# One step of a hybrid DeltaNet / attention network on one core: modulation loads in pieces, gate rows in two heads' memories, softmax scaling on GpSimd or DVE

## The chip, the core and the metric

The kernel runs on one core of a Trainium2 chip. The metric is the device time of one execution in microseconds (us); the time before is the median of 3 runs. Below, PE is TensorE's matmul queue and PEld its weight loads, DVE is VectorE, ACT ScalarE, POOL GpSimd, and SP the engine whose queue issues the DMAs.

## What is computed

Two layers of width 1024 over 384 tokens, 128 of context (`x_prompt`) and 256 latent (`x_sample`). Layer 0 mixes with a gated DeltaNet of 8 heads, layer 1 with windowed attention of 16 heads; each layer ends with a gated feed-forward block. All arithmetic is float32; large products are split into high and low parts and done as three float32r products. Cut to what matters here:

```python
m = silu(cvec) @ w_ada[i] + b_ada[i]              # modulation, (1024) @ (1024, 6144), for context and latent
shift, scale, gate, shift2, scale2, gate2 = split(m, 6)
h = rmsnorm(x, g) * (1 + scale) + shift
y = gated_delta_mixer(h) if i == 0 else attention(h)
x = x + gate * rmsnorm(y, g)
h = rmsnorm(x, g) * (1 + scale2) + shift2
x = x + gate2 * rmsnorm(conv_ffn(h), g)
...
p = softmax(concat([scores, sink]))[..., :-1]     # attention
o = p @ v
```

## The kernel before, in words

**Who sets the order.** The program is written as tasks (Python generators). A task asks for an engine (`yield "P"` for PE, "A" for ACT, "V" for DVE, "G" for POOL, "Q" for SP's queue), for buffers (`Slots`) or for an event; with several letters it takes the engine that can start it first. A planner (`Sched`, L101) plays this through with written-in costs and grants each engine to the task that could start earliest, then by priority (a small number is urgent). The order found is fixed in the program: every engine, SP among them, works through its own list in that order and waits on semaphores, so whatever stands behind a waiting instruction on its engine waits too. The planner lets DMAs through one after the other at 360 GB/s (`DBW`) with a fixed delay (`DL2`). It has no notion of one engine slowing another.

**The stages.** `begin` (L1818) computes the first modulation and starts layer 0's projections. `delta` (L1094) runs the DeltaNet: tiles of 128 output columns of the input projection (`fm`, L400: 24 matmuls of 384 tokens), and beside them one chain per head (`t_chain`, L1257). A chain loads the head's decay rows `dm` as a broadcast (`t_decay`, L1243), forms the matrix `N`, and inverts it in `t_inverse` (L1439), whose way goes through DRAM: `N` is written (`nd<-N`), its diagonal blocks read back (`tmp<-nd`, `X<-nd`), solved on POOL, written (`zd<-inv`) and read in another layout (`x<-zd`) before PE can go on. The convolution of a projected tile (`conv`, L444) frees the bank that the tile was in; `vf` is its output for v. `tm` (L857) does the output projection, holds the last weights back so that the token blocks finish one after the other, and then makes the transition: for each block `y` = result x gate (`t_gated`, L706), x is updated (`t_half`, L735) and multiplied with (1 + g) (`t_scale`, L752), and TensorE multiplies with a diagonal matrix of the norms (`diag,y`) and adds the shift (`t_quarter`, L758). `ffn` (L946) and `attention` (L1573) call the same `tm`.

**Modulation.** `w_ada` comes in 40 loads of 1 MB behind the first ones (`t_ada`, L514), each into one of the buffers in `self.ada`: two of its own at first (`ada`), later any memory that a stage lends (`lend`, L388). Two loads make one step of 512 columns (`t_mod`, L523; its matmuls are `ada,sc`, `head,sc` and so on), which is fitted in between other work with priority 9 or 20; steps 11 and 12, 16 to 18 and 22 and 23 are kept to fill the three transitions. The rows of gate and (1 + g) are written to DRAM (`gdram`, `adram`) and loaded back as broadcasts of 1 MB into all partitions (`t_rows`, L662). At the end of the DeltaNet this happens after the hook (L1142) has waited for every chain, given the chains' memory back and issued the reload of x, whose memory the chains use as scratch. The memories of heads 4 to 7 (`head`) are lent to the modulation when those heads are done (L1408 to 1411).

**Attention.** `t_unit` (L1704) handles two heads of one token block: scores, then a reduction with mask and sink on DVE, the exponentials on ACT, the sum's reciprocal `l`, and the scaling of `P` by it on DVE, one instruction per head (48 in all, 16 of 128 columns and 32 of 384). PE then transposes `P` (`ident,P`), the result is copied to `PT` by ACT or DVE, and multiplied with v.

Of the kernel before, what the change touches and what calls it, by code (L numbers as in the profile page):

```python
# [11 lines left out]
F32 = mybir.dt.float32  # L12
F32R = mybir.dt.float32r
BF16 = mybir.dt.bfloat16
AF = mybir.ActivationFunctionType
ALU = mybir.AluOpType

D = 1024
# [4 lines left out]
H = 8  # L23
# [29 lines left out]
DMIN = 0.06  # L53
DBW = 360.0
DQ = 0.47
SV = 0.0
# [44 lines left out]
class Sched:  # L101
# [17 lines left out]
    def set(self, ev):  # L119
        self.acts.append(lambda end: self._set(ev, end))  # L120

    def put(self, slots, *items):
# [142 lines left out]
class Net:  # L265
# [248 lines left out]
    def t_ada(self):  # L514
        for l, n, half in self.msrc:
            raw = yield self.ada, 1
            yield "Q"
            self.s.put(self.adaful, (raw, self.dma(raw, self.i["w_ada"][l, n, half])))

# [337 lines left out]
    def tm(self, act, ready, plan, l, w, tail, nxt, hook=None):  # L857
# [24 lines left out]
        for n, pieces in enumerate(plan):  # L882
            if n == (len(plan) - tail if hook else 0):
                pool = hook() if hook else self.pool
                if hook:
                    pool = yield from pool
                ctx["gate"] = pool.tile([128, 2, D], F32, name="gate"), Event()
                self.s.spawn(self.t_rows(self.gates[l, w], self.gdram[l][w], *ctx["gate"]), 3)
                if nxt is not None:
                    ctx["arow"] = pool.tile([128, 2, D], F32, name="arow"), Event()  # L890
                    ctx["diags"] = [pool.tile([128, 128], F32, name=f"diag{b}") for b in range(3)]
                    ctx["shift"] = [pool.tile([128, n], F32R, name=f"shift{n}{m}") for m, n in enumerate((128, 128, 16))], Event()
                    self.s.spawn(self.t_shift(self.AB[nxt], *ctx["shift"]), 3)
                    self.s.spawn(self.t_rows(self.AB[nxt], self.adram[nxt[0]][nxt[1]], *ctx["arow"]), 3)
            wt = yield self.wready, 1
# [198 lines left out]
    def delta(self, pool, nxt):  # L1094
        tc, i, s = self.tc, self.i, self.s
        with ExitStack() as late:
# [17 lines left out]
                   for n in range(NB)]  # L1114
# [6 lines left out]
            self.norms = Slots([dict(osb=t(f"osb{n}", [128, 3, 128]), **{k: t(f"{k}{n}", [128, 3]) for k in ("so", "rt", "rs")})  # L1121
                                for n in range(2)])
            self.odone = odone = [[Event()] for _ in range(H)]
            self.gateh, self.written = set(), set()
# [17 lines left out]
            def hook():  # L1142
# [8 lines left out]
                yield "Q"  # L1151
                self.load_x()
                return pp

# [102 lines left out]
    def t_chain(self, h, t):  # L1257
# [150 lines left out]
        if h < H - 4:  # L1408
            s.put(self.hslots, t)
        else:  # L1410
            self.lend(t["mem"].rearrange("p (j c) -> p j c", j=4))
# [292 lines left out]
    def t_unit(self, ti, b, q, done):  # L1704
# [4 lines left out]
        w = yield self.Ps, 1  # L1709
# [26 lines left out]
        for hh in range(2):  # L1736
            V.tensor_scalar(P[:, hh, :n], P[:, hh, :n], l2[:, hh:hh + 1], None, op0=ALU.mult)
        PT = []
# [230 lines left out]
```

## Time and profile before

| | us |
|---|---|
| runs | 1107.46, 1107.84, 1106.46 (median 1107.46) |
| the profiled execution, its own time | 1107.74 |
| its span, from the first to the last instruction | 1106.0 |
| PE busy in the span | 1062.2 (96%) |
| DVE, ACT, POOL busy | 696.2, 549.8, 235.0 |
| DMA moved | 177.86 MB, mean 161 GB/s |

Busy time is that in which an engine has an instruction in work. PE pipelines its matmuls, so a busy PE can still be at less than its peak. PEclk is the clock that was granted to TensorE as a share of 2.4 GHz, averaged over a stretch in which it can only be at 1.2 or 2.4. In a timeline, the number in brackets behind a row is how long the engine had stood idle before it and what ended that.

### The profile page before, as it was taken

Reading aid. Unit: us, or ns where it says so; the run is one execution under the profiler, and the core shown is the slowest. Engines: PE = TensorE matmul, PEld = TensorE weight load, DVE = VectorE, ACT = ScalarE, POOL = GpSimd, SP = SyncE. Lnnn points to the kernel's source line nnn. Section 1 sums busy time; section 2 is a strip of 40 time slices with the busy share of each in tenths; the row PEclk is TensorE's granted clock in tenths of the full one; section 3 lists DMA queues with packets and bytes.
Section 4 is the critical chain, followed back from the end, with each engine's and each line's share of the span. In section 5 each row is a group of like instructions: output and inputs, shape, how many; then the busy total and the mean of one; then the engine's idle time right before and its main releaser. Section 6 shows DMA issues by size and latency. Waiting matters only on the chain.

```text
span 1106.0 us, 19683 instructions
## 1 busy us (share of the span) xinstructions
PE 1062.2 (96%) x7397; PEld 927.4 (84%) x7397; DVE 696.2 (63%) x1685; ACT 549.8 (50%) x1127; POOL 235.0 (21%) x403
## 2 busy tenths in 40 slices
PE   6999899999998999999999999999999999999997
PEld 4887778899785999999988869776769999999886
DVE  5578656988546565656654456878577556566434
ACT  4576754767534444444543345566455444445422
POOL 0023545646202122222200021000031222221000
PEclk9999999999899999999999999998999999999999
DMA  9768664356345534533583346621514434335431
GB/s 364 279 224 293 189 193 127 104 167 204 96 166 223 199 126 132 196 120 128 169 316 126 113 133 220 212 95 41 192 35 142 132 118 132 126 123 172 129 119 57
DMA packets 73567, 177.86 MB, mean 161 GB/s; under 512 B 25816, under 2 KB 38744, under 8 KB 66432
## 3 DMA queue, kind: packets, MB, share of 16 engines
q1 hardware_dynamic: 73472, 176.61, 47.7%
q8 instruction: 58, 0.95, 0.3%
q14 instruction: 37, 0.30, 0.1%
HBM read 169.45 MB, written 7.13 MB: 160 GB/s over the span
## 4 chain that ended last, share of the span: by engine, by line
PE 81%; DMA 6%; DVE 5%; POOL 4%; issue 2%; ACT 1%; SPq 1%; DVEq 0%; POOLq 0%; ACTq 0%
PE bank L299 79%; PE bank L319 2%; POOL tmp L261 1%; DMA tmp<-nd 1%; DVE y L261 1%; POOL inv L261 1%; DMA gate<-gdram 1%; DMA nd<-N 1%; DMA x<-zd 1%; DMA ada<-in_w_ada 1%; DVE x L261 1%; DMA first<-in_w_ada 1%; SPq L324 1%; POOL stat L261 1%; DVE hlo L261 1%
## 5 line engine op out<-in xcount | busy, mean ns | idle before, releaser
L299 PE MATMUL bank<-hhi,whi 128*128 128x384 f32 x832 | 283.8, 341 | 4.1 <-DVE vf L261 2.8
L299 PE MATMUL bank<-hlo,whi 128*128 128x384 f32 x832 | 283.6, 341 | 0.2 <-DVE hlo L261 0.2
L299 PE MATMUL bank<-hhi,wlo 128*128 128x384 f32 x832 | 282.2, 339 | 0.0
L261 DVE TENSOR_TENSOR wlo<-raw,whi 128x1024 fp32r<-128x1024 f32 x151 | 184.9, 1225 | 64.1 <-ACT whi L261 64.0
L261 DVE SCALAR_TENSOR_TENSOR u<-bank,cw_ff,u 128x127 f32<-128x127 f32 x352 | 122.3, 410 | 145.3 <-ACT u L261 145.3
L261 ACT ACTIVATE whi<-raw 128x1024 fp32r<-128x1024 f32 x151 | 158.6, 1052 | 58.3 <-PE bank L299 46.8
L299 PEld LDWEIGHTS bank<-hhi,whi 128*128 128x128 f32 x832 | 156.7, 188 | 14.6 <-DVE vf L261 3.4
L299 PEld LDWEIGHTS bank<-hlo,whi 128*128 128x128 f32 x832 | 156.7, 188 | 4.2 <-issue 2.0
L299 PEld LDWEIGHTS bank<-hhi,wlo 128*128 128x128 f32 x832 | 156.7, 188 | 1.2 <-issue 0.8
L261 ACT ACTIVATE u<-bank,cw_ff 128x384 f32<-128x384 f32 x88 | 59.2, 673 | 177.2 <-PE bank L299 177.2
L261 POOL TENSOR_TENSOR g<-u 128x384 f32<-128x384 f32 x44 | 79.6, 1809 | 307.0 <-DVE u L261 276.6
L299 PE MATMUL bank<-whi,hhi 128*128 128x512 f32 (+1 forms) x246 | 96.7, 393 | 0.0
L299 PE MATMUL bank<-wlo,hhi 128*128 128x512 f32 (+1 forms) x246 | 94.1, 383 | 0.0
L299 PE MATMUL bank<-whi,hlo 128*128 128x512 f32 (+1 forms) x246 | 94.0, 382 | 0.0
L261 POOL TENSOR_TENSOR stat<-stat,mhalf 128x1 f32<-128x1 f32 x24 | 15.7, 656 | 253.0 <-DVE stat L261 253.0
L299 PE MATMUL bank<-hhi,wlol 128*128 128x384 f32 x200 | 67.9, 339 | 0.0
L299 PE MATMUL bank<-hlo,whil 128*128 128x384 f32 x200 | 67.7, 339 | 0.0
L299 PE MATMUL bank<-hhi,whil 128*128 128x384 f32 x200 | 67.7, 339 | 0.0
L261 DVE TENSOR_TENSOR wlol<-raw,whil 128x1024 fp32r<-128x1024 f32 x38 | 46.3, 1218 | 14.0 <-ACT whil L261 14.0
L299 PEld LDWEIGHTS bank<-whi,hhi 128*128 128x128 f32 x246 | 46.6, 190 | 9.6 <-issue 0.7
L299 PEld LDWEIGHTS bank<-whi,hlo 128*128 128x128 f32 x246 | 46.7, 190 | 9.2
L299 PEld LDWEIGHTS bank<-wlo,hhi 128*128 128x128 f32 x246 | 46.8, 190 | 8.0
(253 smaller groups left out, 1740.0 us busy)
## 6 DMA issues: line engine op xcount, KB each, us to landing
raw<-in_ffn_w_up SPq DMA_DIRECT2D x88, 512.0 KB
ada<-in_w_ada SPq DMA_DIRECT2D x32, 1024.0 KB
raw<-in_ffn_w_down SPq DMA_DIRECT2D x44, 512.0 KB
raw<-in_dn_w_in SPq DMA_DIRECT2D x29, 512.0 KB
first<-in_w_ada SPq DMA_DIRECT2D x6, 1024.0 KB
head<-in_w_ada SPq DMA_DIRECT2D x4, 1024.0 KB
raw<-in_dn_w_out SPq DMA_DIRECT2D x8, 512.0 KB
gate<-gdram SPq DMA_DIRECT2D x4, 1024.0 KB
```

Source lines behind the costliest of these rows:

```text
L261: return f(out, *a, **k)
L299: self.nc.tensor.matmul(out, lhsT, rhs, **kw)
L319: self.nc.tensor.transpose(out, src, ident)
L324: self.nc.sync.dma_start(out=out, in_=src)
```

## The change

1. A modulation load of 1 MB becomes four DMAs of 256 KB into the same buffer, and in the planner's time at least 1.5 us pass between the end of issuing one piece and the next of this task.
2. When heads 4 and 5 are done, their memories are no longer lent to the modulation; the rows of gate (into the first that finishes) and of (1 + g) (into the second) are loaded into them, as soon as these rows are in DRAM. The transition after the DeltaNet uses them. In the place where gate and (1 + g) had their own tiles, two buffers `adb` are made after the chains and lent to the modulation. The other transitions keep their own tiles.
3. The scaling of `P` asks for "VG": the planner gives each of the two instructions of a unit to DVE (as before) or to GpSimd, there as a product with a broadcast of the reciprocal.

```diff
@@ -52,6 +52,7 @@
 DL2 = 1.6
 DMIN = 0.06
 DBW = 360.0
+PIECES, PAUSE = 4, 1.5
 DQ = 0.47
 SV = 0.0
 ZD = 1
@@ -118,6 +119,9 @@
 
     def set(self, ev):
         self.acts.append(lambda end: self._set(ev, end))
+
+    def after(self, ev, time):
+        self.acts.append(lambda end: self._set(ev, end + time))
 
     def put(self, slots, *items):
         for i in items:
@@ -514,8 +518,14 @@
     def t_ada(self):
         for l, n, half in self.msrc:
             raw = yield self.ada, 1
-            yield "Q"
-            self.s.put(self.adaful, (raw, self.dma(raw, self.i["w_ada"][l, n, half])))
+            for j in range(0, 4, 4 // PIECES):
+                if j:
+                    yield pause
+                yield "Q"
+                c = slice(j, j + 4 // PIECES)
+                ev, pause = self.dma(raw[:, c, :], self.i["w_ada"][l, n, half][:, c, :]), Event()
+                self.s.after(pause, PAUSE)
+            self.s.put(self.adaful, (raw, ev))
 
     def mod_prio(self):
         return 0 if not self.started else 9 if self.mod_count < self.mod_goal or self.filling else 20
@@ -884,14 +894,18 @@
                 pool = hook() if hook else self.pool
                 if hook:
                     pool = yield from pool
-                ctx["gate"] = pool.tile([128, 2, D], F32, name="gate"), Event()
-                self.s.spawn(self.t_rows(self.gates[l, w], self.gdram[l][w], *ctx["gate"]), 3)
+                if hook:
+                    ctx["gate"], ctx["arow"] = self.lentrows
+                else:
+                    ctx["gate"] = pool.tile([128, 2, D], F32, name="gate"), Event()
+                    self.s.spawn(self.t_rows(self.gates[l, w], self.gdram[l][w], *ctx["gate"]), 3)
+                if nxt is not None and not hook:
+                    ctx["arow"] = pool.tile([128, 2, D], F32, name="arow"), Event()
+                    self.s.spawn(self.t_rows(self.AB[nxt], self.adram[nxt[0]][nxt[1]], *ctx["arow"]), 3)
                 if nxt is not None:
-                    ctx["arow"] = pool.tile([128, 2, D], F32, name="arow"), Event()
                     ctx["diags"] = [pool.tile([128, 128], F32, name=f"diag{b}") for b in range(3)]
                     ctx["shift"] = [pool.tile([128, n], F32R, name=f"shift{n}{m}") for m, n in enumerate((128, 128, 16))], Event()
                     self.s.spawn(self.t_shift(self.AB[nxt], *ctx["shift"]), 3)
-                    self.s.spawn(self.t_rows(self.AB[nxt], self.adram[nxt[0]][nxt[1]], *ctx["arow"]), 3)
             wt = yield self.wready, 1
             for k, _ in pieces:
                 yield full[k]
@@ -1120,6 +1134,7 @@
                                      R=t("R", [128, 2, 128]), sn=t("sn", [128, 2, 128]))])
             self.norms = Slots([dict(osb=t(f"osb{n}", [128, 3, 128]), **{k: t(f"{k}{n}", [128, 3]) for k in ("so", "rt", "rs")})
                                 for n in range(2)])
+            self.lentrows = []
             self.odone = odone = [[Event()] for _ in range(H)]
             self.gateh, self.written = set(), set()
             s.spawn(self.t_zero(nqs, works), 8)
@@ -1150,6 +1165,7 @@
                 s.put(self.wlast, wlast)
                 yield "Q"
                 self.load_x()
+                self.lend(*[pp.tile([128, 4, 512], F32, name=f"adb{n}") for n in range(2)])
                 return pp
 
             self.ahs, self.recycle = Slots(self.hslices()), 0
@@ -1407,6 +1423,11 @@
         yield xc0
         if h < H - 4:
             s.put(self.hslots, t)
+        elif h < H - 2:
+
+            rows, ev = t["mem"].rearrange("p (s d) -> p s d", s=2), Event()
+            self.lentrows.append((rows, ev))
+            s.spawn(self.t_rows(*((self.gates[0, 0], self.gdram[0][0]), (self.AB[0, 1], self.adram[0][1]))[len(self.lentrows) - 1], rows, ev), 3)
         else:
             self.lend(t["mem"].rearrange("p (j c) -> p j c", j=4))
 
@@ -1734,7 +1755,14 @@
         V.tensor_tensor(l2, l2, es, op=ALU.add)
         V.reciprocal(l2, l2)
         for hh in range(2):
-            V.tensor_scalar(P[:, hh, :n], P[:, hh, :n], l2[:, hh:hh + 1], None, op0=ALU.mult)
+            yield "VG"
+            p, l = P[:, hh, :n], l2[:, hh:hh + 1]
+            if s.eng == "A":
+                A.activation(p, p, AF.Copy, scale=l)
+            elif s.eng == "V":
+                V.tensor_scalar(p, p, l, None, op0=ALU.mult)
+            else:
+                self.G.tensor_tensor(p, p, l.to_broadcast([128, n]), op=ALU.mult)
         PT = []
         for hh in range(2):
             p = yield self.PTs, 1
```

**The order on SP, head 0's inverse (layer 0).** Before, from the writing of the inverse (`zd<-inv`) on:

```order
L324 DMA zd_628<-inv 24x16x16 x2
L324 DMA ada_93<-in_w_ada 128x2048
L324 DMA ada_94<-in_w_ada 128x2048
L324 DMA x<-zd_628 128x6x32
L324 DMA tmp<-nd_632 24x16x16
L324 DMA X<-nd_632 24x16x16
```

and with the change:

```order
L328 DMA zd_634<-inv 24x16x16 x2
L328 DMA ada_94<-in_w_ada 128x512
L328 DMA gdram_134<-mrow_100 16x128
L328 DMA x<-zd_634 128x6x32
L328 DMA tmp<-nd_638 24x16x16
L328 DMA X<-nd_638 24x16x16
```

Two whole modulation loads stood between the inverse's way out and its way back; now one piece stands there, and others ahead of them. Over the whole order, three steps of the modulation lie early in the DeltaNet stage as before, and steps 7 to 9 at its end.

**The order on SP around the end of the DeltaNet.** Before, with `x<-in_x` the reload of x behind the last chain:

```order
L324 DMA raw_76<-in_ffn_w_up 128x1024
L324 DMA raw_74<-in_ffn_w_up 128x1024
L324 DMA head_581<-in_w_ada 128x2048
L324 DMA x<-in_x_prompt 128x1024
L324 DMA x<-in_x_sample 128x2x1024
L324 DMA gate<-gdram_134 128x2048
L324 DMA arow<-adram_131 128x2048
L324 DMA raw_75<-in_ffn_w_up 128x1024
```

and with the change, first where the gate rows are, ahead of the last heads' transfers:

```order
L328 DMA ada_93<-in_w_ada 128x512
L328 DMA mdram_128<-modev_95 4x512 x2
L328 DMA head_589<-gdram_134 128x2048
L328 DMA ada_93<-in_w_ada 128x512 x2
L328 DMA raw_74<-in_dn_w_out 128x1024
```

then the rows of (1 + g):

```order
L328 DMA adram_131<-ab_139 16x128
L328 DMA ada_94<-in_w_ada 128x512
L328 DMA head_585<-adram_131 128x2048
L328 DMA ada_94<-in_w_ada 128x512
L328 DMA raw_76<-in_dn_w_out 128x1024
```

and around the reload of x:

```order
L328 DMA raw_74<-in_ffn_w_up 128x1024
L328 DMA head_587<-in_w_ada 128x512
L328 DMA x<-in_x_prompt 128x1024
L328 DMA x<-in_x_sample 128x2x1024
L328 DMA head_587<-in_w_ada 128x512
L328 DMA ada_93<-in_w_ada 128x512
L328 DMA raw_75<-in_ffn_w_up 128x1024
```

The gate rows have moved over 50 rows up, the (1 + g) rows (`head_585<-adram_131`) stand 11 rows ahead of the reload, and neither follows it any more.

**The order on POOL in attention.** Before, where `rc<-xs,rope` belongs to the rotation of q and the two memsets to the coming transition:

```order
L261 TENSOR_TENSOR rc_6292<-xs_6289,rope 128x256
L261 TENSOR_TENSOR rc_6294<-xs_6290,rope 128x256
L261 TENSOR_TENSOR rc_6292<-xs_6289,rope 128x256
L261 MEMSET shift_7101 128x128
L261 MEMSET shift_7102 128x128
L261 TENSOR_TENSOR rc_6294<-xs_6290,rope 128x256
```

and with the change:

```order
L265 TENSOR_TENSOR P<-P,l_6404 128x384 x2
L265 TENSOR_TENSOR rc_6389<-xs_6386,rope 128x256
L265 TENSOR_TENSOR P<-P,l_6408 128x128 x2
L265 TENSOR_TENSOR rc_6391<-xs_6387,rope 128x256
L265 TENSOR_TENSOR P<-P,l_6400 128x128 x2
L265 TENSOR_TENSOR rc_6389<-xs_6386,rope 128x256
L265 TENSOR_TENSOR P<-P,l_6404 128x384
L265 TENSOR_TENSOR rc_6391<-xs_6387,rope 128x256
L265 TENSOR_TENSOR P<-P,l_6412 128x128 x2
L265 TENSOR_TENSOR P<-P,l_6396 128x384
L265 TENSOR_TENSOR rc_6389<-xs_6386,rope 128x256
```

In all, 16 scalings of 128 columns and 10 of 384 are now on POOL; 22 of 384 remain on DVE. DVE has 9 more copies to `PT` of 384 columns, 4 more of 128 and one more of the output `o`, which ACT had before. In PE's order the last head's block product (`Y,x`) stands behind 3 matmuls of the output projection, where it stood behind 15.

## Rows read from the trace of the kernel before

**Rows 1.** The page: busy tenths and GB/s in 40 slices of the span.

```profile
PE   6999899999998999999999999999999999999997
...
GB/s 364 279 224 293 189 193 127 104 167 204 96 166 223 199 126 132 196 120 128 169 316 126 113 133 220 212 95 41 192 35 142 132 118 132 126 123 172 129 119 57
```

**Rows 2.** Busy us of PE, PEld, DVE, ACT, POOL by stretch; PEclk, DMA.

```profile
80.00:160.00 80.00, 72.23 (x733) 57.52 (x731) 55.63 (x162) 53.66 (x128) 38.74 (x111) 0.97 0.71 225
120.00:140.00 20.00, 17.57 (x255) 15.26 (x254) 11.80 (x34) 14.29 (x39) 11.88 (x32) 0.91 0.57 182
280.00:300.00 20.00, 18.17 (x247) 14.80 (x245) 13.45 (x36) 11.14 (x31) 4.20 (x10) 0.83 0.42 121
340.00:360.00 20.00, 15.48 (x103) 10.45 (x104) 17.11 (x37) 12.31 (x28) 8.09 (x8) 0.91 0.42 143
680.00:760.00 80.00, 75.50 (x549) 59.64 (x547) 66.06 (x247) 49.47 (x154) 5.69 (x9) 0.94 0.35 120
740.00:760.00 20.00, 16.08 (x108) 11.99 (x108) 17.98 (x76) 13.36 (x45) 0.73 (x1) 0.74 0.09 28
```

**Rows 3.** Timeline of PE, 98 to 159 us: start, us, what.

```profile
98.84 0.45 PE L299 MATMUL bank<-hhi,whi 128*128 128x384 f32 x1 [1.11 <-DVE vf L261]
...
117.67 0.45 PE L299 MATMUL bank<-hhi,whi 128*128 128x384 f32 x1 [1.65 <-DVE vf L261]
...
126.41 0.77 PE L299 MATMUL bank<-x,N 32*32 32x32 f32 x44 [2.40 <-DMA x<-zd]
...
158.37 1.03 PE L299 MATMUL bank<-ada,sc 128*32 128x512 f32 x4 [1.42 <-DMA ada<-in_w_ada]
```

**Rows 4.** Timeline of DVE at 113 us.

```profile
113.43 1.74 DVE L261 SCALAR_TENSOR_TENSOR dm<-dm,gc,maskt 128x128 f32<-128x128 f32 x6 [2.86 <-DMA dm<-gcdram]
```

**Rows 5.** The chain of waits in order of time: start, us, what.

```profile
117.97 8.39 DMA x<-zd
...
286.96 2.73 DMA x<-zd
...
324.90 12.48 DMA gate<-gdram
```

**Rows 6.** Timelines of DVE and PE, transitions of layer 0 and of attention.

```profile
337.41 1.29 DVE L261 TENSOR_TENSOR y<-bank,gate 128x512 f32<-128x512 f32 x2 [7.57 <-DMA gate<-gdram]
...
338.16 1.06 PE L299 MATMUL bank<-ada,sc 128*32 128x512 f32 x8 [0.23 <-DVE y L261]
343.21 3.48 PE L299 MATMUL bank<-diag,y 128*128 128x128 f32 x16 [3.98 <-DVE diag L261]
...
354.83 2.05 PE L299 MATMUL bank<-diag,y 128*128 128x128 f32 x16 [0.67 <-DVE diag L261]
...
807.66 2.05 PE L299 MATMUL bank<-diag,y 128*128 128x128 f32 x16 [0.16 <-DVE diag L261]
...
821.17 2.05 PE L299 MATMUL bank<-diag,y 128*128 128x128 f32 x16 [1.91 <-DVE diag L261]
```

**Rows 7.** The tile of the modulation loads: issue on SP, ns min/median/max.

```profile
L324 SPq DMA_DIRECT2D ada<-in_w_ada x32: 327/340/1122, 10.9 to 705.9; - x32
```

**Rows 8.** DVE groups at 660 to 780 us; tiles rc, g and q.

```profile
L261 DVE TENSOR_SCALAR P<-P,l 128x384 f32<-128x384 f32 x28 | 10.5, 418 | 0.5
...
L261 DVE TENSOR_SCALAR P<-P,l 128x128 f32<-128x128 f32 x16 | 3.9, 284 | 0.3
L261 DVE COPY PT<-bank 128x384 f32<-128x384 f32 x7 | 3.8, 557 | 5.6 <-PE bank L319 3.6 <-ACT es L261 1.9
...
L261 DVE COPY o<-bank 128x128 f32<-128x128 f32 x9 | 2.6, 287 | 4.4 <-PE bank L299 4.4
...
L261 POOL TENSOR_TENSOR rc<-xs,rope x10: 723/774/900, 663.9 to 748.9; 128x256 f32<-128x256 f32 x10
...
L261 POOL TENSOR_TENSOR g<-u x44: 1017/1858/1863, 370.1 to 1010.5; 128x384 f32<-128x384 f32 x44
...
L261 DVE COPY q<-xs x8: 219/226/772, 672.6 to 748.9; 128x128 f32<-128x128 f32 x8
```

## Prediction

> **What bounds the kernel now.** The prediction starts from the shares of the page: TensorE is busy in almost every slice [rows 1], so an edit pays only where TensorE stands idle or runs at the lower of its two clock levels (1.2 instead of 2.4 GHz). I looked for those places in the busy time by stretches [rows 2], which lists for each the busy time of the engines and then the granted clock: 80 to 160 us (72.2 busy of 80, so 7.8 idle; clock 0.91 at 120 to 140), 280 to 300 us (1.8 idle, clock 0.83), 340 to 360 us (4.5 idle, clock 0.91) and 680 to 760 us (4.5 idle, 3.9 of them in the last 20, with clock 0.74). The change touches all four; the slices of the feed-forward stages are full [rows 1] and are left alone.
>
> The waits of TensorE in time order say why it stood still early [rows 3]: 1.11 and 1.65 us for a bank that the convolution of v frees (`vf`), 2.40 us for a head's inverse coming back from DRAM (`x<-zd`), 1.42 us for a modulation load. All four are DMA in origin. The convolution that freed the second bank was late because DVE had stood 2.86 us at 113 us in its wait for the decay rows [rows 4]; the first has the same cause. The chain of waits shows the queue [rows 5]: `x<-zd`, which brings a head's inverse back, took 8.39 us for head 0, and 2.73 us for the last head, with no modulation load ahead of it. In the order of before two 1 MB modulation loads stand directly ahead of `x<-zd`. At the page's early rate of 364 GB/s [rows 1] a load of 1.05 MB holds the queue 2.9 us, two 5.8, which is the excess (8.39 less 2.73 is 5.66).
>
> At 324.90 us the gate rows are issued behind the reload of x, and take 12.48 us [rows 5]; DVE waits 7.57 us for them and TensorE 3.98 us [rows 6].
>
> **The change, part by part.**
>
> *Pieces.* 40 loads become 160, each a quarter (0.26 MB, 0.7 us at 364 GB/s), with at least 1.5 planned us between a buffer's pieces. In the order, one piece instead of two loads now stands between `zd<-inv` and `x<-zd` of head 0, so its queue falls by about 5 us, more than the 2.40 us that TensorE waited. The decay rows lose similar neighbours, and the 1.42 us goes because modulation steps 7 to 9 are planned later. Full removal is worth 1.11 + 1.65 + 2.40 + 1.42 = 6.6 us. The clock in 120 to 140 us was 0.91, so about 2 x 0.09 x 20 = 3.6 us at half rate, worth up to 1.8 us: upper end 8.4 us gained. The other end is a loss: 17 pieces (4.5 MB) and the gate rows now lie among the transfers of the last two heads, where before lay two whole loads, and TensorE waits for the last chain at 280 to 300 us. One piece and one weight load of 0.52 MB now stand between its `zd<-inv` and `x<-zd` (0.79 MB, 2.2 us), two pieces between its `nd<-N` and `tmp<-nd` (1.4 us): up to 3.6 us lost if nothing were gained. I take three quarters of 6.6 us, because a wait that goes usually shows part of the next: **5.0 us gained**. The 120 added issues cost SP about 0.34 us each [rows 7], 41 us over the run. I cost that at nothing: it hides in the time in which SP waits for buffers anyway, and if that cover failed, a weight load would be late by one issue, 0.34 us.
>
> *Rows early.* Gate and (1 + g) go into the memories of heads 4 and 5, long before they are needed, and no longer queue behind x. What remains is the transition that the other layers show. From the end of the last out-projection matmul to the end of the last diagonal product it took 337.93 to 356.88 us here, 18.95 us; at the attention layer's end, where the gate was there, 807.50 to 823.22 us, 15.72 us [rows 6]. Difference: **3.2 us gained**. Next in line is x, which is issued at the same place in the plan but with less ahead of it; it was not seen late. Ends: 4.0 us (TensorE's whole wait) and 1.0 us (if x or the second row load, whose modulation step now comes late, is the next wait). Two new buffers go to the modulation in place of heads 4 and 5, so its loads have as many places as before. I cost that at nothing: the loads are issued some 10 us before the transition's modulation steps, which only fill TensorE's pauses; if that cover failed, such a wait would look like the 1.42 us of rows 3.
>
> *Scaling.* The order shows 26 of the 48 scalings of attention on GpSimd: all 16 of 128 columns and 10 of 384. DVE did these at 3.9 us for 16 and 10.5 for 28 [rows 8], so it is freed of 3.9 + 10 x 0.375 = 7.7 us. The planner spends that at once: 9 copies of 384 columns, 4 of 128 and one more of the output move from ScalarE to DVE, 9 x 0.54 + 5 x 0.29 = 6.3 us [rows 8]. Net DVE gains 1.4 us. GpSimd takes 0.72 us for 256 columns and 1.02 for 384 when alone [rows 8], so I estimate 0.42 for 128: 10 x 1.02 + 16 x 0.42 = 16.9 us of new work on it. Its latency in one unit grows by 0.6 us. The rows also show the two engines in each other's way: GpSimd's product of two SBUF tiles has a median of 1.86 us against 1.02 alone, and DVE's copy of q has a median of 0.23 and one case of 0.77 us [rows 8]. What it may bring at most is TensorE's loss there, 4.5 us idle, plus half of 2 x 0.26 x 20 = 10.4 us at the lower level: 9.7 us. What it may cost at most is under the rivals. I take **1.0 us gained**, near DVE's net 1.4, since the relief of ScalarE and the added holds are of like size.
> The Trainium skill, "SBUF — State Buffer", section "Who interferes with whom", says that a DVE instruction with two SBUF inputs, or in a 2-port mode, and a GpSimd instruction that reads SBUF exclude each other for a whole instruction. The trace agrees (1.02 against 1.86 us). By that rule this part alone could lengthen the stage: the third rival.
>
> **Sum.** 1107.7 us (profiled execution, span 1106.0 and 1.7 around it) less 5.0, 3.2 and 1.0 is 1098.5 us. That execution lies 0.3 us above the median of the runs, 1107.5, which the rounding covers.
>
> **The rivals.**
> 1. *Attention gains as well.* DVE is busy 17.98 of 20 us at 740 to 760 us [rows 2], the last units follow each other on it, and ScalarE's lighter load may free their exponentials. With 8 instead of 1 us: 1091.5 us. Against it: most of DVE's relief is spent on copies. Chance 0.17.
> 2. *The early waits only move.* The order keeps each engine's queue strict, and the loads taken out of 60 to 160 us come back beside the last heads. If the 5.0 us are given back at 280 to 300 us, and the rows bring 2 to 3 us: about 1105 us, at the edge of what a measurement can tell. For it: that stage has idle time and a clock of 0.83 already [rows 2]. Against it: the last chain is also planned 12 out-projection matmuls earlier (its block product `Y,x` after 3 instead of 15 of them). Chance 0.19. If in addition the rows are not early in effect, it is no change.
> 3. *GpSimd holds DVE up.* Place: the units from 680 to 760 us. If every one of 26 scalings makes a DVE instruction wait for its whole length, DVE loses 16.9 us against 1.4 freed, 15.5 net; less 8.2 of the other parts that is 7.3 us slower, 1115 us. It decides from the point at which more than 9.6 of the 16.9 us fall on DVE instructions on the units' path. For it: the split of weights, the rotation and the small sums of DVE read two SBUF tiles. Against: its reductions and its copies out of banks read one SBUF tile at most, and it was idle for 14 of 80 us there [rows 2]. With two thirds to all of the holds it is 1109 to 1115 us; I price it at 1112 us. Chance 0.14.
>
> **How the numbers follow.** The forecast has 0.50, with 1092 to 1104 us as its own range from the bounds above. A measurement of this kernel tells about 0.2%, or 2.2 us, from no change. Faster by more (under 1105.3): 0.48 of the forecast, 0.17 of the first rival, 0.08 of the second, 0.01 of the third, 0.74 in all. Same: 0.02, 0.10 and 0.02, which is 0.14. Slower: 0.01 and 0.11, 0.12. The range that holds 8 in 10 leaves out the upper half of the third rival and the lower tip of the first: 1089 to 1110 us.
>
> **What would show it.** Right: head 0's `x<-zd` and `nd<-N` under 5 us; no TensorE wait over 1 us for `vf`, `x<-zd` or a modulation load before 200 us; no DVE wait for `head<-gdram`, and 15 to 16.5 us from the last out-projection to the last diagonal product; the stretch of the last attention units no longer than before. Wrong: a longer wait for the last head's `x<-zd`, a DVE wait for x or `head<-adram` at the transition, or DVE's two-input instructions (the split of 1024 columns, now 1.22 us) well above their durations while GpSimd scales.

## The result and the profile after

The change makes the kernel slower by 0.6%: 1113.70 us, median of 4 runs (1112.21 to 1117.04), against 1107.43 us before; the ratio is 1.0063, 95% interval 1.0044 to 1.0082. A second comparison in this study gave 1.0063 again (1.0039 to 1.0087). The forecast was 1098.5 us. The profiled execution took 1113.49 us, its span is 1111.7 us.

The page of the changed kernel, shares of the span and DMA queue (packets, MB, share of 16 engines):

```profile
PE 1061.8 (96%) x7397; PEld 926.3 (83%) x7397; DVE 700.7 (63%) x1678; ACT 543.5 (49%) x1107; POOL 252.1 (23%) x429
...
q1 hardware_dynamic: 90752, 176.61, 49.7%
```

TensorE's busy time is that of before to 0.4 us (1062.2, 1061.8), so in this profile the 5.7 us by which the span grew are time in which it stood still. In the second profile of the changed kernel (span 1113.5 us) it is busy 1067.3 us, so there most of the growth is busy time. The busy time by stretches answers to [rows 2]:

```profile
80.00:160.00 80.00, 71.76 (x792) 63.42 (x792) 62.26 (x184) 50.26 (x130) 46.45 (x113) 1.00 0.60 165
120.00:140.00 20.00, 16.63 (x233) 14.53 (x233) 13.97 (x35) 12.86 (x36) 12.52 (x29) 1.00 0.66 183
280.00:300.00 20.00, 12.63 (x210) 10.29 (x208) 8.85 (x31) 6.85 (x22) 2.25 (x6) 0.91 0.46 128
340.00:360.00 20.00, 16.65 (x112) 11.57 (x110) 14.98 (x30) 10.90 (x26) 8.11 (x8) 1.00 0.66 219
...
740.00:760.00 20.00, 17.98 (x120) 13.43 (x118) 18.79 (x71) 11.71 (x39) 4.14 (x9) 0.77 0.54 173
```

At 120 to 140 us the clock is 1.00 (0.91 before). Over 80 to 160 us TensorE stands still for 8.2 us, where it was 7.8: the early waits were exchanged, not removed. At 280 to 300 us, where DeltaNet's last inverse comes back, TensorE is busy 12.63 us instead of 18.17: the largest new hole. The transition (340 to 360) and attention's end (740 to 760) are better than before. Its timeline names the waits, as [rows 3] and [rows 6] did:

```profile
76.62 3.42 PE L303 MATMUL bank<-ada,sc 128*32 128x512 f32 x14
82.65 1.05 PE L303 MATMUL bank<-ada,sc 128*32 128x512 f32 x2 [2.61 <-DMA ada<-in_w_ada]
...
107.99 1.05 PE L303 MATMUL bank<-ada,sc 128*32 128x512 f32 x2 [1.37 <-DMA ada<-in_w_ada]
...
134.17 0.71 PE L303 MATMUL bank<-x,N 32*32 32x32 f32 x48 [2.45 <-DMA x<-zd]
...
288.56 0.80 PE L303 MATMUL bank<-x,N 32*32 32x32 f32 x48 [3.73 <-DMA x<-zd]
...
299.62 0.86 PE L323 MATMUL bank<-ident,osb 128*128 128x128 f32 x3 [2.73 <-DVE osb L265]
...
343.39 2.05 PE L303 MATMUL bank<-diag,y 128*128 128x128 f32 x16 [0.41 <-DVE diag L265]
...
351.48 2.05 PE L303 MATMUL bank<-diag,y 128*128 128x128 f32 x16 [1.20 <-DVE diag L265]
...
358.00 2.05 PE L303 MATMUL bank<-diag,y 128*128 128x128 f32 x16 [1.74 <-DVE diag L265]
```

The waits for `vf` are gone and the transition waits less. The wait for `x<-zd` is not: it was 2.40 us for the first head [rows 3] and is 2.45 us for the second, whose reload took 5.39 us (the chain of waits: start, us, what):

```profile
128.65 5.39 DMA x<-zd
```

New are two waits for the last piece of a modulation load (step 5's 14 first matmuls spread over 3.42 us, then 2.61 us of standing still, where a whole step of 16 takes 1.92 us), and 7.3 us between 284 and 300 us (1.8 before): the two rows of 3.73 and 2.73 us and 0.9 us in small ones. Around the first of these two, TensorE before the change:

```profile
286.69 1.50 PE L299 MATMUL bank<-x,Q 128*128 128x128 f32 x12
288.03 1.03 PE L299 MATMUL bank<-head 128*128 128x256 f32 x4
289.73 0.80 PE L299 MATMUL bank<-x,N 32*32 32x32 f32 x48 [0.67 <-DMA x<-zd]
```

and with the change, behind the row of 288.56 us:

```profile
289.30 2.49 PE L303 MATMUL bank<-x,Q 128*128 128x128 f32 x12
291.58 1.84 PE L303 MATMUL bank<-head 128*128 128x256 f32 x4
```

The last head's `x<-zd` was issued at 284.16 us and used at 288.54, 4.4 us where [rows 5] had 2.73. It was also issued 2.5 us behind the end of issuing `zd<-inv`, where it was 1.5 before: SP issued two small stores of a modulation step (282.96 to 284.05 us) just ahead of it. Before, 2.5 us of products (`x,Q`, `head`) stood ahead of the wait; with the change they stand behind it, and the granted clock over them, after TensorE had stood still for 3.73 us, was 0.65 (1.00 ahead of the wait). DVE through the second wait:

```profile
293.53 1.38 DVE L265 SCALAR_TENSOR_TENSOR osb<-bank,gc,osb 128x128 f32<-128x128 f32 x4 [3.66 <-PE bank L303]
...
295.94 0.79 DVE L265 TENSOR_TENSOR mrow<-mrow 32x256 f32<-32x256 f32 x2
296.77 0.28 DVE L265 TENSOR_TENSOR mrow<-mrow,brow 32x128 f32<-32x128 f32 x1
297.08 0.34 DVE L265 SCALAR_TENSOR_TENSOR ab<-mrow,zero,grow 32x128 f32<-32x128 f32 x1
...
299.28 0.68 DVE L265 TENSOR_SCALAR osb<-osb,rs 128x128 f32<-128x128 f32 x3
```

DVE had to wait for `head`, then worked from 293.53 us on without a pause, also in the rows left out here. Its work on the rows of (1 + g) (`mrow`, `ab`, 1.5 us) and its copies for the last chain stand ahead of the scaling of an earlier head's output (`osb`), and in TensorE's order that output stands ahead of the first matmul of the output projection, so nothing was there to fill the hole. SP issued the small loads for the rows of (1 + g) up to 291.3 us, some of them held until an earlier transfer had landed, but DVE did not wait for them: no idle time stands before its `mrow` rows.

To see where each kernel gains and loses, I cut the span at marks of TensorE's timeline: the end of DeltaNet's transition (start of the last `diag,y`), attention from its first score to the first `diag,y` behind it, and the rest. One value per profile, in us; two where there are two profiles.

| kernel | start to the transition's last `diag,y` | attention | span |
|---|---|---|---|
| before | 354.83 | 126.39 | 1106.0 |
| changed | 358.00, 359.72 | 126.61, 126.63 | 1111.7, 1113.5 |
| pieces alone | 356.61 | 130.12 | 1112.9 |
| rows alone | 352.29, 349.74 | 132.41, 132.40 | 1111.1, 1106.9 |
| scaling alone | 353.90 | 128.93 | 1107.6 |
| rows and scaling | 350.13, 348.95 | 125.68, 125.69 | 1102.2, 1099.4 |

Up to the first mark TensorE does the same number of matmuls in every kernel. Of the 5.7 us, 3.2 lie before that mark, 0.2 in attention, 0.6 between the two, and 1.7 behind attention (300.0 us to the end, 298.3 before), which the last section puts down to the clock.

### The profile page after: what moved, and what is told of

It reads as the page before. It is cut to its first block, busy times and chain, and to the rows that moved or that the text cites. A ratio compares the mean times of both kernels' runs of the same rounds, so it can differ in the third digit from the quotient of the medians.

```text
span 1111.7 us, 19926 instructions
## 1 busy us (share of the span) xinstructions
PE 1061.8 (96%) x7397; PEld 926.3 (83%) x7397; DVE 700.7 (63%) x1678; ACT 543.5 (49%) x1107; POOL 252.1 (23%) x429
## 3 DMA queue, kind: packets, MB, share of 16 engines
q1 hardware_dynamic: 90752, 176.61, 49.7%
## 4 chain that ended last, share of the span: by engine, by line
PE 78%; DVE 7%; DMA 6%; POOL 4%; issue 3%; SPq 1%; ACT 1%; POOLq 0%; DVEq 0%; ACTq 0%
PE bank L303 76%; DMA first<-in_w_ada 2%; PE bank L323 2%; POOL tmp L265 1%; POOL inv L265 1%; DVE x L265 1%; DVE y L265 1%; SPq L328 1%; DMA ada<-in_w_ada 1%; DVE hlo L265 1%; POOL stat L265 1%; DMA nd<-N 1%; DVE P L265 1%; DMA x<-zd 0%; DMA dm<-gcdram 0%
```

## The experiments

Ratios are to the kernel before, run on the same chip in the same session, with the 95% interval.

**Each part alone, and the change without the pieces.** Pieces alone, from before:

```diff
+PIECES, PAUSE = 4, 1.5
...
+            for j in range(0, 4, 4 // PIECES):
```

> Only the first part of the change: the modulation loads in four paced pieces. Theory A (the pieces make it slower): PE shows the waits for ada of the changed kernel again, 2.6 and 1.4 us near 82 and 108 us, the steps 7 to 9 stay at the end of the DeltaNet, and PE stands still for about 5 us between 284 and 300 us; the transition stays as long as before (18.95 us). Time 1107.4 + 5 to 9, so 1112 to 1116 us. Rival B (the rows brought in early hold up the last heads): without them the stretch from 280 to 300 us is no worse than before (idle about 1.8 us), and the time is 1100 to 1108 us.

Measured: 1115.67 us, 1.0085 (1.006 to 1.011). Theory A for the time; but the hole at 280 to 300 us is 2.6 us here, and with early rows and whole loads 2.5, so the big hole needs pieces and early rows together. The profile is 6.9 us longer than the one before: 1.8 up to the first mark, 3.7 in attention, most of the rest between them.

Rows alone, from the changed kernel:

```diff
-PIECES, PAUSE = 4, 1.5
+PIECES, PAUSE = 1, 1.5
...
-            yield "VG"
...
+            V.tensor_scalar(P[:, hh, :n], P[:, hh, :n], l2[:, hh:hh + 1], None, op0=ALU.mult)
```

> Only the second part: gate and (1 + g) rows early in the buffers of heads 4 and 5, loads whole, scaling on DVE. Theory A: the wait for gate (7.57 us of DVE, 3.98 us of PE at 343 us before) goes, nothing else changes, time 1107.4 - 1 to 3, so 1104 to 1106.5 us. Rival B: the two row loads and the work on the (1 + g) rows lie in the last solve's stretch, PE is idle there for some 5 us as in the changed kernel, and the time is 1109 to 1114 us.

Measured: 1108.90 us, 1.0025 (1.001 to 1.004). Neither theory: DeltaNet and its transition gain as forecast, and attention, which the edit does not touch, gets 6.0 us longer.

Scaling alone, from before:

```diff
-            V.tensor_scalar(P[:, hh, :n], P[:, hh, :n], l2[:, hh:hh + 1], None, op0=ALU.mult)
+            yield "VG"
...
+                self.G.tensor_tensor(p, p, l.to_broadcast([128, n]), op=ALU.mult)
```

> Only the third part: attention's scaling on GpSimd or DVE. Its order differs from before only in attention and behind it. Theory A: attention (660 to 800 us) gains 0 to 1.5 us, time 1106 to 1107.5 us. Rival C (GpSimd holds DVE): DVE's idle time shrinks but its operations grow longer, attention loses 1 to 5 us, time 1108 to 1112 us.

Measured: 1108.99 us, 1.0017 (1.0005 to 1.0029), attention 2.5 us longer. These are rival C's numbers; whether GpSimd is the cause is taken up below.

Rows and scaling, without pieces:

```diff
-PIECES, PAUSE = 4, 1.5
+PIECES, PAUSE = 1, 1.5
```

> The changed kernel with PIECES = 1, so whole modulation loads, with the early rows and the new scaling. Theory A: faster than both, 1107.4 - 1 to 4, so 1103.5 to 1106.5 us. Rival B: about as slow as the changed kernel, 1109 to 1114 us.

Measured: 1103.94 us, 0.9975 (0.9956 to 0.9994). It beats both kernels, the one before by 0.6 to 4.9 us. The pieces therefore cost 9.4 us alone (0.85%) and 9.7 us on top of the other parts (1.0063 over 0.9975). Attention in these kernels, busy time from its first score to the first `diag,y` behind it; before:

```profile
681.27:807.66 126.39, 121.62 (x832) 95.06 (x831) 97.95 (x338) 73.28 (x218) 8.53 (x12) 0.96 0.37 127
```

rows alone, and its second profile:

```profile
678.76:811.17 132.41, 124.67 (x832) 96.07 (x831) 101.03 (x345) 70.44 (x211) 8.52 (x12) 0.95 0.36 121
```

```profile
674.59:806.99 132.40, 124.78 (x833) 96.04 (x832) 101.03 (x345) 70.51 (x211) 8.55 (x12) 0.95 0.36 121
```

scaling alone, then rows with scaling:

```profile
678.75:807.68 128.93, 125.10 (x833) 97.76 (x832) 96.17 (x325) 68.23 (x203) 26.83 (x40) 0.95 0.35 124
```

```profile
676.60:802.28 125.68, 121.08 (x833) 95.42 (x832) 95.11 (x323) 69.19 (x207) 25.53 (x38) 0.97 0.36 128
```

The same matmuls (832 or 833 recorded) take 125.7 to 132.4 us, one kernel repeats its value to 0.02 us, and in none of these does TensorE wait for a DMA there. Where no transfer is waited for, attention's length goes with the order that the planner found.

**Other transfers in the same order.** A piece is cut by partitions:

```diff
-                c = slice(j, j + 4 // PIECES)
-                ev, pause = self.dma(raw[:, c, :], self.i["w_ada"][l, n, half][:, c, :]), Event()
+                c = slice(32 * j, 32 * (j + 4 // PIECES))
+                ev, pause = self.dma(raw[c], self.i["w_ada"][l, n, half][c]), Event()
```

> The changed kernel with its pieces cut the other way: a piece is 32 partitions of the tile with all their 8 KB each, not 128 partitions with 2 KB each. The pieces are as large, the planner's costs and so the order on every engine are the same. Theory P (the transfers themselves suffer, since 2 KB packets take longer: the DMA engines were busy 24.9 us longer for the same bytes): that extra goes, the waits of PE for ada at 82.7 and 108.0 us shrink below 1 us each, the reload x<-zd near 288 us comes back towards 2.7 us, and the time is 1105 to 1110 us. Theory L (the steps 7 to 9 and the head solves stand at bad places in the order): the same 1111 to 1115 us, with the stretch from 284 to 300 us as it was (PE idle 6 to 7 us).

Measured: 1119.84 us, 1.0120 (1.0101 to 1.0139). The cut made transfers dearer, not cheaper: the queue's share of the engines rose to 55.2% for the same 176.61 MB (49.7% in the changed kernel; over all runs here 47.3 to 48.7 with whole loads in DeltaNet and behind, 48.7 to 50.4 with most loads in 2 KB pieces), and packets fell to 75,392, so the number of packets does not set the price. It lies above both theories' ranges, but answers the question from the other side: with every engine's order held, slower pieces alone cost some 6 us more. Rates (last column, GB/s) at 41 to 44 us, with the engines full and the modulation loads issued from 37.6 us on in the queue; before:

```profile
41.00:44.00 3.00, 3.00 (x19) 3.00 (x19) 2.59 (x9) 1.86 (x4) 0.00 (x0) 1.00 1.04 433
```

changed:

```profile
41.00:44.00 3.00, 3.00 (x19) 3.00 (x18) 2.31 (x7) 1.86 (x4) 0.00 (x0) 1.00 1.04 378
```

by partitions:

```profile
41.00:44.00 3.00, 3.00 (x21) 2.92 (x20) 1.76 (x8) 1.39 (x5) 0.00 (x0) 1.00 1.03 203
```

433, 378 and 203 GB/s; the planner reckons with 360 for all three. TensorE's wait for step 5 became

```profile
79.88 1.06 PE L303 MATMUL bank<-ada,sc 128*32 128x512 f32 x8 [1.62 <-DMA ada<-in_w_ada]
86.19 1.94 PE L303 MATMUL bank<-ada,sc 128*32 128x512 f32 x8 [5.25 <-DMA ada<-in_w_ada]
```

**The steps early, no pause, and both edits.** First the steps early:

```diff
-        return 0 if not self.started else 9 if self.mod_count < self.mod_goal or self.filling else 20
+        return 0 if not self.started else 9
```

> The changed kernel with one number of the planner changed: modulation steps always have priority 9, not 20 until their goal, which puts the steps 7 to 10 back between 386 and 512 of the 792 projection matmuls of DeltaNet (672 to 771 and the output projection in the changed kernel). The pieces are as they were. Theory L: the row chain of the steps is gone from the last solve's stretch, PE is idle there for 2 to 3 us instead of 7.3, and the time falls to 1104 to 1109 us. Theory P: the waits of PE for the pieces stay and some more come, 1110 to 1117 us.

Measured: 1121.50 us, 1.0140 (1.0116 to 1.0163), above both theories. The hole before 300 us went, but the heads' chains, now behind the steps, came later: TensorE waited 5.7 us in all for `x<-zd` and 4.1 us for `head`, and the transition ended at 367.15 us.

No pause:

```diff
-PIECES, PAUSE = 4, 1.5
+PIECES, PAUSE = 4, 0.0
```

> The changed kernel with PAUSE = 0: pieces without the pause between them. The steps 7 to 9 then stand at 456, 672 and 713 of the 792 matmuls. Theory P: the transfers stay as slow, PE's waits for ada stay within 1 us of the changed kernel's, 1110 to 1116 us. Theory L: partly better, since step 7 is early again, 1107 to 1112 us. A third reading (the pauses alone make the last piece late): the wait at 82.7 us goes, 1106 to 1110 us.

Measured: 1111.23 us, 1.0053 (1.0032 to 1.0074): by the median about 1 us better than the changed kernel, which the intervals do not separate. The wait of 2.61 us shrank to 1.25 and the one of 1.37 went, so the pauses are a part of those two waits, but 3.00 us for `vf` came in their place.

Priority 9 together with the cut by partitions, both diffs as above:

> Both edits of the two runs before together: pieces by partitions, steps at priority 9. If both theories hold a part of the loss, their gains add up, and the time is 1100 to 1106 us; if one alone holds it, this run equals the better of the two within 2 us.

Measured: 1138.03 us, 1.0288 (1.0261 to 1.0316): neither of the two readings. Over the changed kernel that is about 25 us, more than the 6 and 9 us of the two edits alone. Attention took 136.63 us; with the same order on every engine and the pieces of the change (the run of the steps early) it took 127.39. Here transfers set its length, not the order: TensorE waited 8.4 us for modulation pieces in it, most of it once:

```profile
709.46 1.93 PE L303 MATMUL bank<-ada,sc 128*32 128x512 f32 x8 [7.68 <-DMA ada<-in_w_ada]
```

**Pieces for some steps only.** `pieces` replaces `PIECES` in the loop:

```diff
+            pieces = PIECES if 12 * l + n > 10 else 1
```

and for the other two runs `< 7` and `7 <= 12 * l + n <= 10`.

> The changed kernel with whole loads for the steps 4 to 10 and pieces from step 11 on; the steps stand in DeltaNet where they did before. If the pieces cost their time in DeltaNet (the wait of PE for step 5 at 76 to 84 us, the last solve's stretch from 284 to 300 us), the stretch from 80 us to the first matmul of the transition takes 255 to 258 us as with whole loads (255.5, against 263.4 in the changed kernel), and the time is 1103 to 1106 us. If the loss lies in the pieces of the later stages, it stays at 1109 to 1114 us.

Measured: 1105.42 us, 0.9991 (0.9979 to 1.0003); first matmul of the transition at 336.19 us. Without pieces in DeltaNet its loss is gone.

> The changed kernel with pieces for the steps 4 to 6 only, whole loads from step 7 on. If the late landing of the first steps' last piece is what counts, PE's wait in step 5 near 82 us stays, DeltaNet takes 3 to 5 us longer than with whole loads, and the time is 1107 to 1110 us. If the last solve's stretch is what counts, and the steps 8 and 9 (now at 672 and 707) still stand in front of it, it shows PE idle of 5 us or more between 280 and 300 us, and 1109 to 1113 us; without that idle, 1104 to 1107 us.

Measured: 1109.17 us, 1.0019 (1.0004 to 1.0034). The wait for step 5 stayed (2.27 us at 83.9 us), yet the transition began at 335.86 us, as with whole loads (335.52): that wait takes the place of others (`vf`, `head`) and is paid by them. Attention took 128.93 us; its order on TensorE is row for row that of scaling alone, which took 128.93 us too. The profiled execution, 1106.01 us, is the second fastest of 12, so the profile understates the median by 3 us.

> The counterpart of the run with pieces up to step 6: pieces for the steps 7 to 10 only, the rest whole. PE has no wait for a piece before 100 us. If the first steps' landing is what counts, the time is 1103 to 1106 us; if the last solve's stretch counts (step 9 at 672, step 10 at the end of the 792), it is 1107 to 1112 us, with PE idle of 4 us or more between 270 and 300 us.

Measured: 1105.78 us, 0.9993 (0.9979 to 1.0008); transition from 335.99 us. Pieces in one half of DeltaNet's steps cost DeltaNet nothing that these single profiles show; in all of them, 8 us.

**The planner's price.**

```diff
-        ev = self.s.dma(4 * math.prod(out.shape))
+        ev = self.s.dma(4 * math.prod(out.shape) * price)
```

with 1.5 for pieces.

> The changed kernel, its pieces charged 1.5 times their bytes in the planner's table (a rate of 240 instead of 360 GB/s; 331 was measured where the queue was full). PE's order now has step 5 at 240 and step 6 at 456 of the 792 matmuls, not at 216 and 312. If the planner's low price is what costs the time, PE's waits for ada shrink below 1 us together, and the time is 1106 to 1110 us. If pieces cost by what they do to the order at the end of DeltaNet (the steps 7 to 9 stand at 624, 699 and 760), it is 1111 to 1117 us, with the lost time between 260 and 300 us.

Measured: 1113.67 us, 1.0077 (1.0051 to 1.0103). The waits for pieces went, as wanted, and new ones came where the order had changed:

```profile
96.34 0.69 PE L303 MATMUL bank<-hhi,whi 128*128 128x384 f32 x1 [4.32 <-DVE head L265]
...
333.78 0.78 PE L323 MATMUL bank<-ident,osb 128*128 128x128 f32 x3 [4.09 <-DVE osb L265]
```

**The last hole alone.**

```diff
+            pieces = PIECES if 12 * l + n != 10 else 1
```

> The changed kernel with whole loads for step 10 alone. The order on every engine is the changed kernel's up to 282 us; from there SP issues two loads of 1 MB in place of eight pieces, the eight small row loads stand close together, and DVE's work on the (1 + g) rows stands behind the scaling of head 6's output, not ahead of it. If that stretch is the main part of the loss, PE's idle time between 284 and 300 us falls from 7.3 to 2 to 3 us, the transition's first matmul comes at 337 to 340 us (343.4 in the changed kernel), and the time is 1107 to 1110 us. If the loss lies in DeltaNet's earlier waits (the piece of step 5 at 82.7 us and what follows), the first matmul stays at 342 to 345 us, and the time at 1112 to 1115 us.

Measured: 1112.38 us, 1.0045 (1.0025 to 1.0064), the transition from 341.63 us. The transition lies between the two expectations, the time at the lower edge of the second. DVE's row work no longer stands in front, but TensorE now meets step 10 in the hole and waits for its loads:

```profile
288.42 1.06 PE L303 MATMUL bank<-ada,sc 128*32 128x512 f32 x8 [2.00 <-DMA ada<-in_w_ada]
292.19 1.93 PE L303 MATMUL bank<-ada,sc 128*32 128x512 f32 x8 [2.70 <-DMA ada<-in_w_ada]
```

4.7 us, and 0.5 in small waits, for 7.3. With rows and scaling and whole loads the same stretch holds output-projection matmuls ahead of `osb`:

```profile
291.88 0.62 PE L303 MATMUL bank<-x 32*32 32x32 f32 x48 [1.14 <-DVE x L265]
292.43 0.50 PE L303 MATMUL bank<-whi,hhi 128*128 128x512 f32 x1
...
295.40 0.63 PE L323 MATMUL bank<-ident,osb 128*128 128x128 f32 x3 [0.75 <-ACT Y L265]
```

**Second profiles,** of unchanged kernels.

> A second profile of the rows alone, with nothing changed. If its slowness is attention's order, attention (first scores to the transition behind it) takes over 130 us again (132.4 in the first profile, 126.4 before); if it was that one run, it takes 125 to 128 us, and the span is 1104 to 1107 us.

> A second profile of the changed kernel and its time beside the other runs of this study. The stall between 284 and 300 us and the wait for the piece of step 5 repeat within 1 us; the time is 1111.5 to 1115 us.

> A second profile of rows with scaling, whole loads. DeltaNet ends and the transition begins at 335 to 338 us again; attention takes 124 to 129 us; span 1099 to 1105 us.

Measured, in this order: 1108.65 us (one run), 1114.59 us at 1.0063, 1101.16 us (one run). Attention took 132.40, 126.63 and 125.69 us, each within 0.02 us of the first profile. The changed kernel's waits repeated (1.96 us at 82.4, 3.93 and 2.73 us at 290 to 301). What moves between executions is DeltaNet, by 1 to 3 us, and the clock.

## Why the prediction was wrong, point by point

**Pieces: 5.0 us gained, it said; 9.4 to 9.7 us lost.** This is the step that failed. Of its removals some came true: head 0's reload was issued at 106.03 us and used at 109.06, 3 us where [rows 5] had 8.39; the waits for `vf` [rows 3] and the low clock at 120 to 140 us are gone. But the wait for `x<-zd` went from the first head to the second (2.40 and 2.45 us), and the waits for pieces (2.61 and 1.37 us) took the place of the rest, so of the 6.6 us nothing was gained over 80 to 160 us beyond the clock. Three things were missing. First, a piece was priced rightly by itself (0.7 us; at the 378 GB/s measured with the engines full it is the same), but there was no term for the landing of the last of four paced pieces: each step was planned on TensorE before it (the two waits for `ada`). This alone seems to be paid by the waits it replaces, as the run with pieces up to step 6 shows. Second, the line "the 1.42 us goes because modulation steps 7 to 9 are planned later" booked a move as a saving. The steps came back at the end of DeltaNet with their row work on DVE. The bound for that place, 3.6 us, counted only the transfers ahead of a head's `x<-zd` and `tmp<-nd`; for `x<-zd` that part held (1.6 us longer, of 2.2). It left out 1.0 us by which SP issued this load later, TensorE's own order there (the products behind the wait, the output projection behind `osb`) and DVE's row work ahead of `osb`. The hole grew by about 5.5 us (7.3 against 1.8). Third, attention: in the run with pieces alone its new order made it 3.7 us longer (0.2 in the changed kernel). The sign that the prediction gave for being wrong, a longer wait for the last head's `x<-zd`, is there: 3.73 us for 0.67.

The 120 added issues, costed at nothing, took 382 ns each by the median (340 in [rows 7]). What SP's issuing shows in the hole, the 1.0 us above, is that of the stores which came along with the steps.

The second rival, "the early waits only move", named the mechanism and the place, and was some 9 us too low: it had the 5.0 us given back at 280 to 300 us; there 5.5 us were lost, but the 5.0 had not been gained before.

**Rows early: 3.2 us gained, it said.** Right up to the transition: the four profiles with whole loads and early rows end it at 348.95 to 352.29 us, mean 350.3, the two without at 354.83 and 353.90, mean 354.4: 4.1 us gained, with a spread that does not tell it from 3.2. About 2 us of it is TensorE's standing still (from 310 us to that mark 3.3 us with early rows, 5.5 and 5.1 without); the rest goes with the clock, which over that stretch was 1.00 with early rows, 0.96 and 0.92 without, and for which the forecast had no term of its own. The forecast's 15 to 16.5 us can't be compared: from the last out-projection matmul to the end of the last diagonal product it is 11.7 us, because nine of these matmuls now stand behind the first diagonal products. DVE's 7.57 us for the gate rows [rows 6] are gone; it waits 0.80 us, for ACT:

```profile
335.35 0.69 DVE L265 TENSOR_TENSOR y<-bank,head 128x512 f32<-128x512 f32 x1 [0.80 <-ACT junk L265]
```

No modulation wait came at the transition, as was costed. But rows alone are 0.25% slower, because attention's order changed with them and took 6.0 us more. With the new scaling it took another order, and the gain stayed.

**Scaling: 1.0 us gained, it said.** Its work was sized well: 15.7 us on GpSimd for 16.9 estimated, and DVE's busy time in attention is 97.56 us for 97.95. Attention in the changed kernel is 0.2 us longer. GpSimd's two groups in attention, then DVE's:

```profile
L265 POOL TENSOR_TENSOR P<-P,l 128x384 f32<-128x384 f32 x10 | 9.6, 968 | 11.8 <-DVE l L265 7.9 <-ACT P L265 1.9 <-PE bank L303 1.0
L265 POOL TENSOR_TENSOR P<-P,l 128x128 f32<-128x128 f32 x16 | 6.1, 401 | 48.2 <-DVE l L265 43.3 <-ACT o L265 4.9
```

```profile
L265 DVE TENSOR_SCALAR P<-P,l 128x384 f32<-128x384 f32 x22 | 9.1, 441 | 0.2
```

The third rival, GpSimd holding DVE up, did not come about: DVE's scaling of 384 columns went from 418 ns [rows 8] to 441, half a us over 22 of them, its split of 1024 columns from 1219 to 1222 ns, that of 384 columns from 553 to 633, 0.6 us over 8. The rule of the Trainium skill, "SBUF — State Buffer", section "Who interferes with whom", allows such holds; here they are worth about 2.3 us over all of DVE's instructions in attention (the rotation's two products add 1.0, the small sums 0.3), where the rival needed 9.6. In the run of scaling alone, where attention is 2.5 us longer, DVE's instructions grew by 1.7 us (the scaling of 384 columns to 459 ns); in rows with scaling they grew by 1.6 us (455 ns), and attention is 0.7 us shorter than before. So the holds do not decide its length; the order that the planner found does: scaling alone 2.5 us longer, and in the company of the rows 6.7 us shorter. One reading of the rows was off: the longest copy of q [rows 8], 0.77 us, is no single case; three of the eight took 0.75 us or more.

**The range, 1089 to 1110 us,** had no case in which attention is planned anew. Its length over the kernels here runs from 125.0 to 132.4 us where TensorE waits for no DMA in it, more than any one term of the sum. In the changed kernel itself this came to 0.2 us, which is luck: the miss lies before the first mark, 3.2 to 4.9 us later where 8.2 us earlier was forecast, and 1.7 us in the clock of the last stage.

**Still open.** Why pieces in all of DeltaNet's steps cost 8 us there, and in either half none, is not settled: the last hole is about 5 us of it, and filling that hole otherwise gave back 2. And no run shows which move of the order makes attention longer.

## What to carry to other kernels

Where a planner fixes the order, an edit's direct saving is one term and the new order of everything behind it another; here the second was 3.7 us (pieces) and 6.0 us (rows) in attention, where neither was aimed, so each part has to be timed alone and together. A load that is cut up lands when its last piece does: ask what stands behind that landing on the waiting engine, and where the work goes that used to fill the gap. A step that "is planned later" is not gone; find the place it now shares.

## What was not expected of the hardware

The shape of a transfer sets its rate at equal size: 256 KB as 128 partitions of 2 KB ran at 378 GB/s, as 32 partitions of 8 KB at 203 to 216, with the engines full. The Trainium skill, "DMA: Bandwidth & Descriptors", section "Specifications", gives 512 B as the least transfer for line rate; the rows of both cuts, 2 and 8 KB, are above it, so by that line alone both should run at the full rate. The measurement decides: neither reached the 433 GB/s of the whole load.

TensorE's clock takes or leaves some 1.7 us behind a transition. In the changed kernel, 824 to 832 us, behind 1.90 us of standing still:

```profile
824.00:828.00 4.00, 2.82 (x15) 2.82 (x16) 0.96 (x3) 0.60 (x1) 0.55 (x1) 0.71 0.01 4
828.00:832.00 4.00, 4.00 (x24) 2.68 (x24) 1.32 (x3) 2.63 (x4) 0.00 (x0) 0.86 0.01 2
```

The third number from the end, 0.71 and 0.86, costs (0.29 + 0.14) x 4 = 1.7 us. Before, at the same place and behind 1.91 us of standing still [rows 6]:

```profile
820.00:824.00 4.00, 2.83 (x24) 2.02 (x24) 1.25 (x4) 1.19 (x2) 0.55 (x1) 1.00 0.01 4
824.00:828.00 4.00, 4.00 (x26) 3.86 (x23) 2.71 (x3) 2.49 (x3) 0.00 (x0) 1.00 0.02 6
```

From the first `diag,y` behind attention to the end it is 300.0 us in the changed kernel and 298.3 before. This is no property of the change: the two profiles of rows with scaling, one program, have 299.9 and 298.3 us there. Over the 18 profiles of this study TensorE stood still for 1.90 to 1.91 us at this place each time; in 12 the clock fell behind it (299.9 to 300.4 us), in 6 it stayed at the upper level (298.3 to 298.4).
